# Attention in slots of 64 queries over 192 keys with the sink as a score column, and x norms summed by ScalarE from a copy of x by tokens

## The chip, the cores and the metric

The kernel runs on one core of a Trainium2 chip. The metric is the device time of one execution in microseconds. The engines are called as the profile calls them: PE (TensorE, with PEld for its weight loads), ACT (ScalarE), DVE (VectorE), POOL (GpSimd) and SP (SyncE, which issues nearly all DMAs). L245 is line 245 of the kernel; where the changed kernel is meant, the text says so, since its lines are shifted.

## The reference, cut to what matters

Two pre-norm residual layers over 4096 tokens of 1024 features in float32, and a last norm. Layer A is sliding-window attention: 16 query heads in 4 groups, each with one key/value head, 64 features a head, a window of 128 keys, and one learned sink per head. Layer B is a pooling mixer. Both are gated by SiLU(z).

```
def attn_layer(h, w_in, sinks, w_out):            # h = rmsnorm(x, g)
    q, k, v, z = split(h @ w_in)                  # 1024, 256, 256, 1024 columns
    o = swa_with_sinks(q, k, v, sinks)
    return (o * silu(z)) @ w_out                  # added to x

# swa_with_sinks, per block of 128 queries and 256 keys (block before, own block)
s = einsum('bnqhgd,bnkhd->bnhgqk', qb, kc) / sqrt(64)
diff = qi + 128 - kj
s = where((diff >= 0) & (diff < 128) & not_pad, s, -inf)
m = max(max(s), sink)
p = exp(s - m);  p = p / (sum(p) + exp(sink - m))
o = einsum('bnhgqk,bnkhd->bnqhgd', p, vc)
```

## The kernel before, in words

**Products.** Accuracy is that of float32: each operand is split into a high and a low part of a rounded 32-bit type, and a product takes three passes (high·high, high·low, low·high). A unit is 256 output columns of a projection for one group of 512 tokens: 48 matmuls of 128x512 (`in_piece`, L245), for v 96 of 128x256 (`v_piece`, L255).

**Order.** Layer A goes through 8 groups. A group is 14 units: k, q0 to q3 (one per kv head), v, z0 to z3, and the four out units of the group before. Beside them run 16 attention iterations, one for each kv head j and block b of 128 queries: `it_scores`, then `it_turn` (transposes of the probabilities), then `it_pv`. All work is put into a list of events with a due time in units (`at(t, fn, ...)`, offsets in the dictionary `T`), which is sorted and emitted in that order; each engine executes its part of it in order. Accumulators and scores live in PSUM: `mm` (two buffers) for the units, `pt` (two buffers) which the transposes, the PV result and the norm sums share, and `s` (one buffer) for the scores.

**Scores.** `it_scores` makes for each of the 4 heads of j a 128x256 score tile by two matmuls (L338: q high and low stacked in the 128 rows, against k high and then k low, which stand in both halves of `kt`). The window holds exactly 128 of the 256 keys, so DVE writes the block before over the masked half (`copy_predicated`, L344) and only 128 columns go on: DVE takes the maximum (L349) and the negative bias with the sink (L350), ACT the exponentials with their sums (L353), DVE and ACT add the sink's exponential (L354 to L356), POOL multiplies by the reciprocal (L358).

**PV.** `it_turn` transposes the 4 tiles into one `pt` buffer (L365), ACT rounds it (L371), DVE takes the low parts (L372, L376), and POOL zeroes by `affine_select` (L382 to L386) the keys that belong to the other block. `it_pv` multiplies with v: two matmuls of 512 columns (L396) and two of 256 (L398, L399).

**Norms.** A group's x is loaded by features (`xt`, 4 DMAs of 512 KB, L163). For the norm of the next group ACT squares 8 chunks, DVE adds them (L178), the sum is split, and PE sums over the features with a matrix of ones (`total`, L198, two matmuls); two small DMAs bring the result into another shape, `spread` (L205) makes the reciprocal root and broadcasts it by two further DMAs. Then `x_scale` (DVE) and `h_chunk` (ACT, DVE) make h. The output of layer A goes through the same `square`, `rstd`, `total` and `spread` (keys 8 to 15) for the norm of layer B.

**Layer B** follows from about 1610 us on in 4 pairs of groups. What prepares its first pair (loads of x, `h_load`; `h_scale`; the sums that its products need, `factor`) is placed within the last units of layer A.

## Time and profile before

| | us |
|---|---|
| median of 3 runs | 2634.66 (2632.97 to 2638.23) |
| the profiled execution | 2637.84 |
| its span | 2635.8 |
| PE busy | 2542.3 (96%) |
| DVE busy | 1796.4 (68%) |
| ACT busy | 1082.9 (41%) |
| POOL busy | 661.7 (25%) |

How to read it: a row of a timeline gives the start and the length of a run of equal instructions on one engine, then engine, line, operation, tiles written and read, the shape and xcount; what stands in brackets is the idle time before it and who ended it. A row of the groups gives busy time, the mean of one in ns, and the idle time before. The modelled end of a matmul overlaps the next one's start, so a pace is read from start to start.

### The profile page before, as it was taken

The page shows a single profiled execution, that of the slowest core. Times are in us where ns is not written, and L with a number is a line of the kernel's source. Part 1 is how long each engine was busy: PE and PEld are TensorE (multiplying, and loading weights), DVE is VectorE, ACT ScalarE, POOL GpSimd, SP SyncE. Part 2 cuts the span into 40 slices and gives each one's busy share as a digit, 9 for nine tenths or more (in the row PEclk, how much of TensorE's full clock was granted, in tenths as well). Part 3 has the DMA queues.
Part 4 walks back from the last instruction along what each step waited for, and adds up shares of the span by engine and source line. Part 5 has one row for each costly group of instructions (what it writes and reads, how often), then busy time and mean ns, then how long its engine had stood idle before and what let it go on. Part 6 is the DMA issues. An engine that isn't in the chain of part 4 may idle for free. (4 is left out here: it accounts for less than half of the span.)

```text
span 2635.8 us, 35629 instructions
## 1 busy us (share of the span) xinstructions
PE 2542.3 (96%) x12362; PEld 2120.9 (80%) x12362; DVE 1796.4 (68%) x3074; ACT 1082.9 (41%) x2774; POOL 661.7 (25%) x1048
## 2 busy tenths in 40 slices
PE   7999999999999999999999999999999999999997
PEld 5878878878888788778788877888878877887886
DVE  6898778778777678677677667547645655655544
ACT  5556455455455455455455443123313231331221
POOL 0354444344354354444344340000000000000000
PEclk9999999999999999999999999999999999999998
DMA  7755765775775774765775547667678668758752
GB/s 280 291 190 188 260 226 186 265 234 185 261 263 187 244 244 178 258 231 175 261 236 178 187 166 287 198 206 259 195 251 275 221 220 284 257 180 274 245 203 96
DMA packets 166284, 594.66 MB, mean 226 GB/s; under 512 B 22981, under 2 KB 33221, under 8 KB 137434
## 3 DMA queue, kind: packets, MB, share of 16 engines
q1 hardware_dynamic: 166106, 592.40, 65.8%
q8 instruction: 98, 1.61, 0.2%
q14 instruction: 80, 0.66, 0.1%
HBM read 474.81 MB, written 117.53 MB: 225 GB/s over the span
## 5 line engine op out<-in xcount | busy, mean ns | idle before, releaser
L245 PE MATMUL mm<-h,w 128*128 128x512 f32 x3456 | 853.8, 396 | 2.8 <-DVE sz L321 1.9
L245 PEld LDWEIGHTS mm<-h,w 128*128 128x128 f32 x3456 | 634.7, 190 | 125.2 <-DVE sz L321 2.4
L245 PE MATMUL mm<-a,w 128*128 128x512 f32 x1536 | 368.9, 394 | 5.1 <-DMA w<-wparts 5.1
L245 PEld LDWEIGHTS mm<-a,w 128*128 128x128 f32 x1536 | 285.0, 189 | 61.9 <-DVE xr L729 5.5
L358 POOL TENSOR_TENSOR P<-P,sm 128x512 f32<-128x512 f32 x128 | 140.6, 1099 | 452.6 <-DVE sm L357 340.9
L353 ACT ACTIVATE P<-s,nm 128x128 f32<-128x128 f32 x512 | 180.9, 366 | 130.1 <-DVE nm L350 126.0
L384 POOL TENSOR_SCALAR_AFFINE_SELECT m<-m 64x512 fp32r<-64x512 f32 x256 | 187.5, 733 | 82.7 <-DVE m L376 80.0
L712 POOL TENSOR_TENSOR rs<-ms,mhalf 128x4 f32<-128x4 f32 x7 | 7.0, 1006 | 738.4 <-DVE ms L711 738.4
L382 POOL TENSOR_SCALAR_AFFINE_SELECT m<-m 64x256 fp32r<-64x256 f32 x256 | 110.7, 432 | 276.7 <-ACT m L371 268.3
L338 PEld LDWEIGHTS s<-kt,q 128*128 128x128 f32 x1024 | 140.0, 191 | 39.0 <-ACT P L353 19.2
L338 PE MATMUL s<-kt,q 128*128 128x256 f32 x1024 | 152.0, 287 | 16.9 <-ACT P L353 11.7
L404 ACT COPY tmp<-po 64x256 f32<-64x256 f32 x256 | 93.9, 367 | 149.2 <-DVE o L405 93.0
L405 DVE TENSOR_TENSOR o<-po,tmp 64x256 f32<-64x256 f32 x256 | 107.7, 421 | 45.1 <-ACT tmp L404 39.0
L386 POOL TENSOR_SCALAR_AFFINE_SELECT m<-m 64x256 fp32r<-64x256 f32 x256 | 134.1, 524 | 13.5
L290 DVE TENSOR_TENSOR q<-mm,q 64x512 fp32r<-64x512 f32 x128 | 88.1, 688 | 62.0 <-ACT q L289 59.9
L289 ACT CAST q<-mm 64x512 fp32r<-64x512 f32 x128 | 74.3, 581 | 103.2 <-DVE q L290 57.6
L376 DVE TENSOR_TENSOR m<-pT,m 64x256 fp32r<-64x256 f32 x256 | 107.9, 422 | 7.9
L344 DVE COPY_PREDICATED s<-mask,s 128x512 f32<-128x512 int8 x124 | 85.6, 690 | 36.2 <-PE s L338 35.1
L353 ACT ACTIVATION_READ_ACCUMULATOR P<-s,nm 128x1 f32 x512 | 104.5, 204 | 0.0
L372 DVE TENSOR_TENSOR m<-pT,m 128x512 fp32r<-128x512 f32 x128 | 88.1, 688 | 21.5 <-ACT m L371 17.8
L178 DVE TENSOR_TENSOR sq<-sq,sr 128x512 f32<-128x512 f32 x112 | 87.9, 784 | 20.1 <-ACT sr L177 18.0
L371 ACT CAST m<-pT 128x512 fp32r<-128x512 f32 x128 | 75.4, 589 | 58.2 <-PE pT L365 31.1
(356 smaller groups left out, 4617.8 us busy)
## 6 DMA issues: line engine op xcount, KB each, us to landing
w<-wparts SPq DMA_DIRECT2D x196, 1024.0 KB
wparts<-w SPq DMA_DIRECT2D x28, 1024.0 KB
xt<-in_xt SPq DMA_DIRECT2D x32, 512.0 KB
res<-in_xt SPq DMA_DIRECT2D x32, 512.0 KB
x<-res SPq DMA_DIRECT2D x32, 512.0 KB
xr<-x SPq DMA_DIRECT2D x32, 512.0 KB
w_u<-part_u SPq DMA_DIRECT2D x56, 256.0 KB
w_z<-part_z SPq DMA_DIRECT2D x56, 256.0 KB
```

The lines of the kernel that those rows point to most:

```text
L245: nc.tensor.matmul(ps[:, c], w[:, wl, k % 4, 128 * c:128 * c + 128], rhs(k, hl), start=(k == 0 and i == 0), stop=(k == NK - 1 and i == 2))
L290: nc.vector.tensor_sub(q[64 - r:128 - r, h], src, f32(q[r:r + 64, h]))
L338: nc.tensor.matmul(ps[:, h], qs[s, j][:, h, 128 * b:128 * b + 128], kt[:, j, hl, 128 * b:128 * b + 256], start=(hl == 0), stop=(hl == 1))
L353: nc.scalar.activation(P[:, h], sc[:, h], AF.Exp, bias=nm[:, h:h + 1], scale=SCALE, accum_out=sm[:, h:h + 1])
L358: nc.gpsimd.tensor_mul(P, P, sm.unsqueeze(2).to_broadcast([128, 4, 128]))
L372: nc.vector.tensor_sub(m1[:, 1], pv, f32(m1[:, 0]))
L376: nc.vector.tensor_sub(m2[other, :, cols], pv[own, :, cols], f32(m1[own, 0, :, cols]))
L382: nc.gpsimd.affine_select(out=m2[own, :, cols], in_=f32(m1[own, 0, :, cols]), compare_op=ALU.is_ge, fill=0.0, **keep)
L384: nc.gpsimd.affine_select(out=mv, in_=f32(mv), compare_op=ALU.is_ge, fill=0.0, **drop)
L386: nc.gpsimd.affine_select(out=mv, in_=f32(mv), compare_op=ALU.is_ge, fill=0.0, **keep)
L404: nc.scalar.copy(tmp[d:d + 64], pv[e:e + 64, :, r])
L405: nc.vector.tensor_add(o[d:d + 64, :, 128 * b:128 * b + 128], pv[d:d + 64, :, r], tmp[d:d + 64])
```

## The change

1. **Scores in slots.** A slot is 64 queries of two heads, against the 192 keys that their windows can reach. An iteration has 4 slots (two pairs of heads, two halves of the block) and still 8 matmuls, of 192 columns instead of 256. q is evacuated times -1/8, so scores are negative; ACT writes minus the sink as one more column beside each slot's 128 kept columns; a minimum over 129 columns gives the bias, and the exponentials' sums hold the sink. L350, L354, L355 and L356 go.
2. **PV.** Six matmuls of 256 columns in place of two of 512 and two of 256. The copies of v that this needs are made by POOL (`vn`), ACT and two DMAs a group; the second half of `kt` is filled by 4 DMAs a group in place of ACT and DVE copies.
3. **Norms of x.** For groups 1 to 7, x is loaded a second time by tokens (`xm`, 4 DMAs of 512 KB a group), and ACT squares each with its sum (`accum_out`). The DVE adds, the split, the `total` matmuls and the two small DMAs go for them. The `xt` pool has 2 buffers instead of 4; two of a group's four `xt` are loaded in the last unit, and the scaling of chunks 4 to 7 stands at the end of the unit or after it.
4. **Order.** q2 stands before the last out unit and q3 before z1 in groups 1 to 6; scores are spaced evenly by about 0.8 unit; the norm sums of the output stand 0.9 unit after the end of out3 and no longer at 9.45 units after the group's start.
5. **Start and first pair of B.** The constants are loaded earlier; the preparation of B's first pair is spaced by 6 units for each of its four parts.

The core of the diff:

```diff
+    def xm_load(s, b):
+        t = sp.tile([128, D], F32, tag="xt", bufs=2, name=f"xm{s}_{b}")
+        nc.sync.dma_start(t, xm[s, b])
+        xts[s, "m", b] = t
+
+    def xm_square(s, b):
+        if b == 0:
+            rss[s] = const.tile([128, NB], F32, tag="mr", bufs=2, name=f"mr_{s}")
+        t = xts.pop((s, "m", b))
+        nc.scalar.activation(t, t, AF.Square, accum_out=rss[s][:, b:b + 1])
...
+    def k_twice():
+        for r in (0, 1):
+            v = f32(kt).rearrange("p (c r) l t -> p r c l t", r=2)[:, r]
+            for l in range(2):
+                nc.sync.dma_start(v[64 - 64 * r:128 - 64 * r, :, l, 128:], v[64 * r:64 * r + 64, :, l, 128:])
...
-            nc.scalar.copy(q[r:r + 64, h], src)
-            nc.vector.tensor_sub(q[64 - r:128 - r, h], src, f32(q[r:r + 64, h]))
+            src = ps[r:r + 64, h // 2].rearrange("p (t x) -> p t x", x=64)
+            dst = q[:, h // 2, :, h % 2]
+            nc.scalar.mul(dst[r:r + 64], src, -SCALE)
+            nc.vector.scalar_tensor_tensor(dst[64 - r:128 - r], src, -SCALE, f32(dst[r:r + 64]), op0=ALU.mult, op1=ALU.subtract)
...
     def it_scores(s, j, b):
         ps = rpsum.tile([128, 4, 256], F32, tag="s", bufs=1, name=f"s{s}_{j}_{b}")
-        for h in range(4):
-            for hl in range(2):
-                nc.tensor.matmul(ps[:, h], qs[s, j][:, h, 128 * b:128 * b + 128], kt[:, j, hl, 128 * b:128 * b + 256],
-                                 start=(hl == 0), stop=(hl == 1))
...
+        nc.scalar.copy(view(ps, 1, [(512, 2), (447, 2)]), nsink[:, j].unsqueeze(2).to_broadcast([128, 2, 2]))
+        for c in range(2):
+            for u in range(2):
+                t = 128 * b + 64 * u
+                for hl in range(2):
+                    nc.tensor.matmul(ps[:, 2 * c + u, 2 - 2 * u:194 - 2 * u], qs[s, j][:, c, 2 * b + u].rearrange("p r x -> p (r x)"), kt[:, j, hl, t:t + 192],
+                                     start=(hl == 0), stop=(hl == 1))
...
+        nc.vector.tensor_reduce(mx.rearrange("p (c u) -> p c u", c=2), view(ps, 1, [(512, 2), (319, 2), (1, 129)]), axis=AX.X, op=ALU.min)
+        P = sp.tile([128, 4, 136], F32, tag="P", bufs=2, name=f"P{s}_{j}_{b}")
+        for i in range(4):
+            nc.scalar.activation(P[:, i, 0:129], view(ps, 1 + 512 * (i // 2) + 319 * (i % 2), [(1, 129)]), AF.Exp,
+                                 bias=mx[:, i:i + 1], scale=-1.0, accum_out=sm[:, i:i + 1])
...
-        for hl in range(2):
-            nc.tensor.matmul(po, vm[:, b, j], m1[:, hl].rearrange("p h q -> p (h q)"), start=(hl == 0), stop=False)
-        ph = po.rearrange("p (h q) -> p h q", h=4)
-        nc.tensor.matmul(ph[:, :, 0:64], vp[:, b, j], m2[:, :, 0:64], start=False, stop=False)
-        nc.tensor.matmul(ph[:, :, 64:128], vc[:, b, j], m2[:, :, 64:128], start=False, stop=True)
+        for u, (v, before) in enumerate(((vm, vp), (vn, vq))):
+            for hl in range(2):
+                nc.tensor.matmul(pu[:, u], v[:, b, j], mu[:, u, hl], start=(hl == 0), stop=False)
+            nc.tensor.matmul(pu[:, u], before[:, b, j], m2[:, u], start=False, stop=True)
...
-            order = [("k", 0), ("q", 0), ("v", 0), outs[0], outs[1], ("q", 1), outs[2], outs[3], ("z", 0), ("q", 2),
-                     ("z", 1), ("q", 3), ("z", 2), ("z", 3)]
+            order = [("k", 0), ("q", 0), ("v", 0), outs[0], outs[1], ("q", 1), outs[2], ("q", 2), outs[3], ("z", 0),
+                     ("q", 3), ("z", 1), ("z", 2), ("z", 3)]
...
-            for r, fn in ((9.0, rstd), (9.45, total), (9.75, spread)):
-                at(base + r, fn, NG + s - 1)
+            for r, fn in ((0.1, rstd), (0.9, total), (1.2, spread)):
+                at(base + order.index(("out", 3)) + 1 + r, fn, NG + s - 1)
```

**Where instructions move.** On PE in group 4, from the last products of q1 (`mm` of w_1 with h_7) to the first scores of kv head 1 (`s_1_0`); the `mm` with `a` is an out unit. Before:

```order
L245 MATMUL mm_8887<-h_7_8097,w_1_8817 128x512 x6
L245 MATMUL mm_9032<-a_3_7387,w_0_8894 128x512 x12
L198 MATMUL ms_9047<-sr_8980,ones_r 128x512
L198 MATMUL ms_9047<-sl_8981,ones_r 128x512
L245 MATMUL mm_9032<-a_3_7647,w_0_8894 128x512 x12
L245 MATMUL mm_9032<-a_3_8111,w_1_8972 128x512 x6
L396 MATMUL po_0_3_9081<-m_4_0_3_9005,vm 128x512 x2
L398 MATMUL po_0_3_9081<-m_4_0_3_9006,vp 128x4x64
L399 MATMUL po_0_3_9081<-m_4_0_3_9006,vc 128x4x64
L245 MATMUL mm_9032<-a_3_8111,w_1_8972 128x512 x6
L245 MATMUL mm_9032<-a_3_8550,w_1_8972 128x512 x6
L338 MATMUL s_1_0_9103<-kt,q_1_9023 128x256 x8
```

Now:

```order
L267 MATMUL mm_8515<-h_7_7883,w_1_8431 128x512 x6
L267 MATMUL mm_8667<-a_3_7251,w_0_8522 128x512 x12
L432 MATMUL po_0_2_8703<-m_4_0_2_8613,vm 128x2x128
L375 MATMUL s_1_0_8676<-kt,q_1_8658 128x192 x4
L432 MATMUL po_0_2_8703<-m_4_0_2_8613,vm 128x2x128
L433 MATMUL po_0_2_8703<-m_4_0_2_8614,vp 128x2x128
L432 MATMUL po_0_2_8703<-m_4_0_2_8613,vn 128x2x128 x2
L433 MATMUL po_0_2_8703<-m_4_0_2_8614,vq 128x2x128
L398 MATMUL pT_0_3_8715<-ident,P_0_3_8583 128x128 x4
L267 MATMUL mm_8667<-a_3_7573,w_0_8522 128x512 x2
L375 MATMUL s_1_0_8676<-kt,q_1_8658 128x192 x4
```

Between the end of q1 and the first scores that read it stood 42 matmuls of 512 columns, the norm's two and a PV; now 12 and one of 256. The norm sums of x are gone from the place, and the scores are issued in two halves, one for each pair of heads.

On PE in group 3, around the norm sums of the output (`ms` with `ones_r`). Before:

```order
L338 MATMUL s_1_3_7344<-kt,q_1_6971 128x256 x8
L245 MATMUL mm_7377<-h_0_5928,w_0_7211 128x512 x6
L365 MATMUL pT_1_2_7394<-ident,P_1_2_7268 128x128 x4
L245 MATMUL mm_7377<-h_1_5980,w_0_7211 128x512 x6
L396 MATMUL po_1_1_7417<-m_3_1_1_7295,vm 128x512 x2
L398 MATMUL po_1_1_7417<-m_3_1_1_7296,vp 128x4x64
L399 MATMUL po_1_1_7417<-m_3_1_1_7296,vc 128x4x64
L245 MATMUL mm_7377<-h_2_5999,w_0_7211 128x512 x6
L245 MATMUL mm_7377<-h_3_6010,w_0_7211 128x512 x6
L245 MATMUL mm_7377<-h_4_6019,w_1_7324 128x512 x6
L245 MATMUL mm_7377<-h_5_6028,w_1_7324 128x512 x2
L198 MATMUL ms_7439<-sr_7390,ones_r 128x512
```

Now:

```order
L432 MATMUL po_1_2_7174<-m_3_1_2_7084,vm 128x2x128 x2
L433 MATMUL po_1_2_7174<-m_3_1_2_7085,vp 128x2x128
L432 MATMUL po_1_2_7174<-m_3_1_2_7084,vn 128x2x128 x2
L433 MATMUL po_1_2_7174<-m_3_1_2_7085,vq 128x2x128
L398 MATMUL pT_1_3_7186<-ident,P_1_3_7060 128x128 x4
L267 MATMUL mm_7122<-h_4_5851,w_1_7044 128x512 x6
L267 MATMUL mm_7122<-h_5_5861,w_1_7044 128x512 x6
L267 MATMUL mm_7122<-h_6_5942,w_1_7044 128x512 x6
L267 MATMUL mm_7122<-h_7_5946,w_1_7044 128x512 x6
L220 MATMUL ms_7229<-sr_7131,ones_r 128x512
L220 MATMUL ms_7229<-sl_7132,ones_r 128x512
```

The two `pt` buffers are taken in turn, so the sums need the buffer of the transposes two places ahead (before: `pT_1_2`, with `po_1_1` after it; now: `po_1_2`, with `pT_1_3` after it). 20 matmuls of 512 columns stood between the last user of `pt` and the sums, and 24 do now; a different tile is waited for.

On SP at the end of layer A, from the broadcasts of the first pair's norm (`bch`) on. Before:

```order
L719 DMA bch_16313<-rsq_120 128x512
L719 DMA bch_16313<-rsq_121 128x512
L724 DMA xr_3_16316<-x_0_76 128x1024
L724 DMA xr_3_16316<-x_1_77 128x1024
L724 DMA xr_2_16319<-x_0_76 128x1024
L724 DMA xr_2_16319<-x_1_77 128x1024
L724 DMA xr_1_16322<-x_0_76 128x1024
L724 DMA xr_1_16322<-x_1_77 128x1024
L724 DMA xr_0_16325<-x_0_76 128x1024
L724 DMA xr_0_16325<-x_1_77 128x1024
L422 DMA x_7_83<-res_0_16138 128x1024
L151 DMA w_0_16384<-wparts_0_2862 128x2048
```

Now:

```order
L754 DMA bch_15718<-rsq_120 128x512
L754 DMA bch_15718<-rsq_121 128x512
L759 DMA xr_3_15721<-x_0_76 128x1024
L759 DMA xr_3_15721<-x_1_77 128x1024
L759 DMA xr_2_15752<-x_0_76 128x1024
L759 DMA xr_2_15752<-x_1_77 128x1024
L457 DMA x_7_83<-res_0_15582 128x1024
L158 DMA w_0_15786<-wparts_0_2734 128x2048
L450 DMA res_2_15736<-in_xt 128x1024
L759 DMA xr_1_15815<-x_0_76 128x1024
L759 DMA xr_1_15815<-x_1_77 128x1024
L158 DMA w_1_15838<-wparts_1_2826 128x2048
```

Eight loads of `xr` stood ahead of the next weights (`w_0`); four do now, and the other four stand between later weight loads.

196 lines of the change are left out of this document (99 added, 97 removed).

## The prediction

> **What bounds the kernel now.** I read the page's sums first, then the windows by stage (width; then busy time and instruction count of PE, PEld, DVE, ACT, POOL; granted PE clock; DMA share; GB/s).
>
> ```profile
> span 2635.8 us, 35629 instructions
> PE 2542.3 (96%) x12362; PEld 2120.9 (80%) x12362; DVE 1796.4 (68%) x3074; ACT 1082.9 (41%) x2774; POOL 661.7 (25%) x1048
> ...
> 215.30:1394.00 1178.70, 1148.77 (x5883) 967.73 (x5882) 885.74 (x1729) 598.83 (x1741) 499.75 (x772) 0.99 0.66 226
> 1610.00:2636.00 1026.00, 999.76 (x4414) 824.18 (x4414) 589.72 (x766) 270.48 (x467) 10.16 (x36) 0.99 0.68 226
> ```
>
> PE is busy 1148.77 of 1178.70 us in groups 1 to 6 (the third row), where the change has nearly all its edits; the next engine, DVE, has 885.74 there, 75%. The last row, layer B's 1026 us, is touched only in its first preparation. So the time is the sum of PE's own paces and of the moments at which it waits. The waits, by the view of waits on PE (total, times, longest):
>
> ```profile
> PE ms L198 <- DVE m L376: 12.6, 6, 2.5
> PE s L338 <- ACT P L353: 11.7, 11, 3.0
> PE pT L365 <- DVE m L376: 5.2, 8, 1.5
> PE mm L245 <- DMA w<-wparts: 5.1, 1, 5.1
> PE po L396 <- POOL m L384: 2.7, 5, 1.4
> PE po L396 <- DVE o L405: 1.6, 3, 1.0
> ```
>
> These 38.9 us are all that waits can give back; the paces must give the rest. They come from the timeline, from start to start:
>
> ```profile
> 1001.87 3.00 PE L245 MATMUL mm<-h,w 128*128 128x512 f32 x12
> 1004.70 0.62 PE L396 MATMUL po<-m,vm 128*128 128x512 f32 x2
> ...
> 1019.49 1.12 PE L338 MATMUL s<-kt,q 128*128 128x256 f32 x8
> 1020.45 0.63 PE L396 MATMUL po<-m,vm 128*128 128x512 f32 x2
> ...
> 1021.15 4.47 PE L255 MATMUL mm<-w,h 128*128 128x256 f32 x36
> ```
>
> 512 columns take (1004.70 − 1001.87)/12 = 0.236 us, 256 columns (1020.45 − 1019.49)/8 = 0.120, a whole PV 1021.15 − 1020.45 = 0.70. Halving the columns thus saves 0.116, and each column costs 0.116/256 = 0.00045.
>
> **The change part by part.** The profiled execution took 2637.84, span and 2.0 around it; the median of the runs is 2634.66, so 3.2 are taken off at the end.
>
> *Scores.* 1024 matmuls go from 256 to 192 columns. No row has 192. If columns alone decide, one takes 0.120 − 64 × 0.00045 = 0.091, and the edit gives 1024 × 0.029 = 30 us; if the narrowing gains nothing, 0. What stands between is the weight load that each matmul needs, seen where the moving operand is a single column:
>
> ```profile
> 2609.26 0.98 PEld L770 LDWEIGHTS msl<-ones,sq 128*128 128x128 f32 x8
> 2610.15 1.02 PEld L752 LDWEIGHTS last<-set_3out_B,w_3o 128*128 128x128 f32 x8
> ```
>
> Eight loads with nothing wide beside them step at (2610.15 − 2609.26)/8 = 0.111. I take 0.111, since the new matmul also brings its own 128x128 weights: **−9.2** (0 to −30). The Trainium skill, "TensorE: Matmul & The Clock Gate", section "Back-to-back issue gap", gives sustained paces of about 81 ns at 128 columns and 131 at 512. An estimate by it is 89 ns at 192 columns and −31 us; but this trace has 0.236 at 512. [...]
>
> *PV.* Six of 256 columns take 6 × 0.120 = 0.72 against 0.70, 128 times: **+2.6** (0 to +4 if the strided operand costs 0.01 a PV more).
>
> *Norm sums of x.* Seven groups lose two matmuls of 512: 14 × 0.236 = **−3.3**. The sums of the output stay, and the 12.6 us of the first wait are six times theirs. One of them:
>
> ```profile
> 715.68 0.60 PE L365 MATMUL pT<-ident,P 128*128 128x128 f32 x4
> ...
> 722.73 0.60 ACT L371 CAST m<-pT 128x512 fp32r<-128x512 f32 x1
> ...
> 724.08 0.87 DVE L376 TENSOR_TENSOR m<-pT,m 64x256 fp32r<-64x256 f32 x2
> ...
> 725.10 0.47 PE L198 MATMUL ms<-sr,ones_r 128*128 128x512 f32 x1 [2.19 <-DVE m L376]
> ```
>
> The sums take the `pt` buffer of transposes written at 715.68; ACT reaches their cast only at 722.73, behind a gate and four exponentials, DVE's subtractions end at 724.95, and PE had come 2.19 us earlier. In the new order the sums take the buffer of a PV result, with 24 matmuls of 512, 5.7 us, after the transposes that follow it. Its readers are two copies on ACT and two additions on DVE, in place of a cast and three subtractions. I count 10 of the 12.6 as gone: **−10** (0, if ACT is as late there, to −12.6).
>
> *Score chain and other waits.* Per iteration DVE and ACT do less between scores and exponentials:
>
> ```profile
> L344 DVE COPY_PREDICATED s<-mask,s 128x512 f32<-128x512 int8 x124 | 85.6, 690 | 36.2 <-PE s L338 35.1
> L349 DVE TENSOR_REDUCE mx<-s 128x4 f32<-128x512 f32 x128 | 88.0, 688 | 2.4
> L350 DVE SCALAR_TENSOR_TENSOR nm<-mx,nsink 128x4 f32<-128x4 f32 x128 | 22.4, 175 | 1.6
> L353 ACT ACTIVATE P<-s,nm 128x128 f32<-128x128 f32 x512 | 180.9, 366 | 130.1 <-DVE nm L350 126.0 <-PE mm L245 3.1
> L353 ACT ACTIVATION_READ_ACCUMULATOR P<-s,nm 128x1 f32 x512 | 104.5, 204 | 0.0
> L376 DVE TENSOR_TENSOR m<-pT,m 64x256 fp32r<-64x256 f32 x256 | 107.9, 422 | 7.9
> L178 DVE TENSOR_TENSOR sq<-sq,sr 128x512 f32<-128x512 f32 x112 | 87.9, 784 | 20.1 <-ACT sr L177 18.0
> ```
>
> The selection goes from 4 x 128 to 4 x 64 columns a row, 0.69 to about 0.42 (as L376 with 256 elements), the 0.175 of L350 goes, and ACT's write of the sink, on 128x2x2, stands before the matmuls. It joins ACT's queue: behind it wait the scores, behind them everything on PE. Between score groups there are at least 7.7 us of PE work in the new order, 6.1 in the old (matmuls counted at the paces above), and the chain itself needs 0.42 + 0.69 + 4 × (0.366 + 0.204) = 3.4. DVE loses 49 × 0.784 = 38 us of L178 over the kernel and 128 × 0.27 = 35 of the selection. The other waits, 11.7 + 5.2 + 2.7 + 1.6 = 21.2, are of an engine that comes late by 1 to 3 us; I count not quite half as gone: **−9** (+11 to −21: as much new again, or all).
>
> *A new wait behind q1.* From the last products of q1 to the first scores that read q there were 42 matmuls of 512 and are 12 and one of 256, 3.0 us. Evacuating q takes four ACT casts and four DVE subtractions:
>
> ```profile
> 925.76 0.58 ACT L289 CAST q<-mm 64x512 fp32r<-64x512 f32 x1 [3.22 <-PE mm L245]
> ...
> 927.61 0.58 ACT L289 CAST q<-mm 64x512 fp32r<-64x512 f32 x1
> ...
> 929.26 0.69 DVE L290 TENSOR_TENSOR q<-mm,q 64x512 fp32r<-64x512 f32 x1
> ```
>
> The first pair was done 929.95 − 925.76 = 4.2 us after it began, with other work between; undisturbed it is two casts and a subtraction, some 1.9. The scores come in two halves now, and the first needs one pair: a wait of 0 to 1.2, and some again for the second half. I take 1 us for 6 groups: **+6** (0 to +12).
>
> *Loads of x by tokens.* 28 more transfers of 512 KB. For one of that size:
>
> ```profile
> 389.19 0.33 SPq L163 DMA_DIRECT2D xt<-in_xt  x1
> ...
> 393.63 0.63 ACT L171 ACTIVATE sq<-xt 128x512 f32<-128x512 f32 x1
> ```
> ```profile
> 67.94 1.26 SPq L163 DMA_DIRECT2D xt<-in_xt  x2
> ...
> 73.65 0.63 ACT L177 ACTIVATE sr<-xt 128x512 f32<-128x512 f32 x1 [5.29 <-DMA xt<-in_xt]
> ```
>
> The first landed within 4.4 us, since its square started without a wait; the second, beside the start's other loads, in 5.7. In the new program the squares are emitted 1.5 to 5 us of PE work behind their loads, which have two buffers, and so wait for the square two before. ACT may stand for 1 to 3 us a group, mostly inside the 7.7 − 3.4 = 4.3 us of slack between scores; 7 groups at 0.7: **+5** (0 to +20; a loss of more is the third rival). The `kt` and v copies, six DMAs a group, cost nothing while v's unit (96 matmuls of 256, 11.5 us) and the out units stand ahead of their readers; without that cover they would cost a landing of 4.4 us a group. POOL's 64 new copies find it idle for 679 of 1179 us.
>
> *The tail.* The one DMA wait of 5.1:
>
> ```profile
> 1590.38 6.17 SPq L724 DMA_DIRECT2D xr<-x  x8
> ...
> 1608.37 0.38 SPq L151 DMA_DIRECT2D w<-wparts  x1
> ...
> 1610.42 2.04 PE L245 MATMUL mm<-a,w 128*128 128x512 f32 x4 [5.07 <-DMA w<-wparts]
> ```
>
> Eight loads go ahead of the weights, four now: **−3.5** (0 to −5). The start and the last group's order: **+2** (−3 to +5).
>
> Sum: −9.2 + 2.6 − 3.3 − 10 − 9 + 6 + 5 − 3.5 + 2 = −19.4, that is 2637.8 − 19.4 = 2618.4 profiled, and less 3.2 **2615** in the runs.
>
> **The rivals.**
>
> *R1, columns decide.* The load hides under the matmul before, and 192 columns take 0.091: 20 us more are gained, **2595**. For it: 256-column matmuls at 0.120, with a load each, are 0.009 above the load's step, so columns and loads do overlap. Against: no row with a load for each matmul steps faster than 0.111.
>
> *R2, waits are only renamed.* The sums wait for the next late tile, the new wait behind q1 takes 1 to 2 us a group, and the tail keeps its 5: −9.2 + 2.6 − 3.3 + 10 = 0, **2635**. For it: the six waits at L198 end with the same ACT and DVE that stay in the path. Against: by the rows above DVE alone has 38 + 35 + 22 = 95 us less to do.
>
> *R3, slower: ACT stands at `xm`.* If each 512 KB takes the 5.7 us of the start or more (the DMA share is already 0.66, and the change adds 4 MB a group: 2 of `xm`, 1 of `kt`, 1 of v), ACT waits at each of four squares some 2.5 us, 10 a group. The stretch has one score gap, whose slack of 4.3 covers part; from there on exponentials and casts come late and PE waits for the rest: 5.7 × 7 = 40, **2655**. It decides once a landing exceeds about 4.5 us. Against: 4.4 at 389 with no wait, at a share like today's.
>
> *R4, narrow matmuls in two passes.* The profile shows twice the emitted instructions for some plain float32 products of 128 columns:
>
> ```profile
> L785 PE MATMUL bcl<-ident,rs_l x16: 271/349/583, 2614.6 to 2628.8; 128*128 128x128 f32 x16
> ```
>
> 16 stand there for 8 emitted. Would the rounded type with fewer than 256 columns go the same way, each score matmul would take about 0.22: 1024 × 0.10 more, **2720**. Against: the rounded types are made to avoid just that, and the transposes of 128 columns (L365, x4 for 4) do not double.
>
> **How the numbers follow.** Forecast 0.60 (its own range 2602 to 2629: the ends of the wait terms), R1 0.14, R2 0.13, R3 0.09, R4 0.04. The range 2588 to 2638 takes in the forecast, R1 and R2 whole; above it lie R3 and R4 (0.13), below it R1 together with all waits gone (0.06). A measurement of this kernel tells about 0.2% (5.3 us) from no change. Faster by more: the forecast, R1 and a fifth of R2, 0.77; within: most of R2, 0.10; slower: R3 and R4, 0.13.
>
> **What would show it.** The step of L375 rows, start to start, near 0.111 (0.091 for R1, 0.2 for R4). No L220 row with a wait above 0.5 us. L375 rows that wait for q's second cast or subtraction, some 1 us in each of six groups. ACT squares of `xm` with a DMA named as releaser: under 3 us a group, 10 for R3. PE's busy time down by about 10. DVE's busy time lower by over 95. I am wrong if a wait with a new name on PE sums to more than 15 us, or if layer B's 1026 us change.

## The result: slower by 4.0%

| us | before | after |
|---|---|---|
| median of the runs | 2636.44 | 2741.77 (2732.12 to 2746.55) |
| the profiled execution | 2637.84 | 2741.26 |
| its span | 2635.8 | 2739.2 |

The ratio is 1.0396, with its interval 1.0364 to 1.0427. The forecast was 2615, with a range to 2638: wrong in sign, by 127 us.

The page of the changed kernel, its sums:

```profile
span 2739.2 us, 35678 instructions
PE 2602.2 (95%) x12604; PEld 2159.3 (79%) x12604; DVE 1626.7 (59%) x2546; ACT 1066.1 (39%) x2728; POOL 701.1 (26%) x1122
```

and its windows by stage, with the columns as in the prediction (group 0; the stretch of time that the prediction used for groups 1 to 6; from there to 1668; and the rest, with layer A's last out units and layer B):

```profile
60.00:215.30 155.30, 137.59 (x754) 117.36 (x753) 102.13 (x167) 79.75 (x212) 61.78 (x93) 0.93 0.72 246
215.30:1394.00 1178.70, 1119.17 (x5730) 940.10 (x5729) 706.72 (x1236) 550.08 (x1602) 500.15 (x784) 0.97 0.69 232
1394.00:1668.00 274.00, 260.74 (x1351) 216.57 (x1349) 165.60 (x301) 128.20 (x391) 119.68 (x191) 0.98 0.62 205
1668.00:2739.00 1071.00, 1042.88 (x4568) 849.76 (x4568) 614.29 (x793) 279.44 (x483) 13.67 (x44) 0.99 0.67 226
```

In the second row DVE is down to 706.72 from 885.74 and ACT to 550.08 from 598.83. Part of this is only that less work falls into the same stretch of time. Over the same work, from group 1's first v product to group 7's (1254.0 us after, 1176.6 before), DVE is busy 758.15 us against 885.81 and ACT 583.43 against 598.62: still less, as the change promises. In the second row PE is down as well, to 1119.17 from 1148.77, and its granted clock from 0.99 to 0.97. PE did less in the same time because it stood, and it ran slower after it had stood. The waits on PE (total, times, longest):

```profile
PE s L375 <- ACT s L370: 33.9, 22, 4.7
PE po L432 <- POOL m L417: 14.8, 26, 1.5
PE pT L398 <- DVE m L410: 12.8, 8, 4.2
...
PE mm L277 <- DMA w<-wparts: 10.7, 6, 3.0
...
PE po L433 <- POOL m L419: 3.9, 7, 1.0
...
PE s L375 <- DVE q L315: 2.9, 6, 0.5
```

The 12.6 us of the norm sums (`ms`) are gone. In their place the scores wait 33.9 us for the sink that ACT writes into their tile, where before they waited 11.7 for ACT's exponentials. One such wait, followed back on all engines:

```profile
1001.59 0.83 SPq L533 DMA_DIRECT2D w_u<-part_u  x2
...
1009.12 0.41 ACT L130 CAST part_u<-sum_u 128x256 fp32r<-128x256 f32 x1 [5.71 <-DMA w_u<-part_u]
...
1009.56 0.42 DVE L131 TENSOR_TENSOR part_u<-sum_u,part_u 128x256 fp32r<-128x256 f32 x1 [5.43 <-ACT part_u L130]
1009.87 0.59 ACT L314 ACTIVATE q<-mm 64x512 fp32r<-64x512 f32 x1
...
1012.42 0.37 ACT L387 ACTIVATE P<-s,mx 128x129 f32<-128x129 f32 x1 [0.20 <-DVE mx L384]
...
1014.31 1.05 POOL L390 TENSOR_TENSOR P<-P,sm 128x516 f32<-128x516 f32 x1 [11.23 <-DVE sm L389]
...
1014.96 0.59 ACT L404 CAST m<-pT 128x512 fp32r<-128x512 f32 x1
...
1015.44 0.17 ACT L370 COPY s<-nsink 128x4 f32<-128x4 f32 x1
...
1015.66 1.14 PE L375 MATMUL s<-kt,q 128*128 128x192 f32 x8 [2.45 <-ACT s L370]
```

`part_u` has nothing to do with this iteration. While layer A runs, both kernels split layer B's weights into high and low parts (ACT casts, DVE subtracts, SP stores them to memory for later); a part has one of two buffers, and is free again when its store has landed. The two stores of 1001.59 had not, so ACT, which executes in order, stood 5.71 us at the head of its queue; DVE stood 5.43 behind it, and POOL, which needs the sums of the exponentials, had been idle for 11.23. The late exponentials are followed by a cast and by the sink, and PE waits 2.45 us for it. The parts are the same in both kernels; the stands are not. The view of waits on ACT, after:

```profile
ACT part_u L130 <- DMA w_u<-part_u: 40.1, 13, 5.7
ACT part_z L130 <- DMA w_z<-part_z: 31.3, 12, 5.9
ACT part_o L130 <- DMA wo<-part_o: 26.9, 9, 6.4
ACT xm L186 <- DMA xm<-in_xm: 23.7, 12, 5.1
```

and before:

```profile
ACT part_u L123 <- DMA w_u<-part_u: 23.5, 16, 3.4
ACT part_o L123 <- DMA wo<-part_o: 21.1, 11, 3.9
ACT part_z L123 <- DMA w_z<-part_z: 18.1, 15, 3.4
ACT part_o L123 <- DMA w_z<-part_z: 8.5, 4, 4.0
```

98 us in three rows against 71 in four, and the longest 6.4 against 4.0; with the small rows of that view it is 112 against 80. Of the 73 us that PE waits for other engines from group 1 to the end of layer A, 60 begin within 14 us after ACT or DVE stood at a DMA; before, 24 of 35. These stands and the 14 us behind them cover about 44% of that stretch after and 40% before.

What a long wait costs beyond itself shows in PE's timeline of group 0:

```profile
104.66 1.04 PE L375 MATMUL s<-kt,q 128*128 128x192 f32 x8
105.53 0.42 PE L432 MATMUL po<-m,vm 128*128 128x256 f32 x2
...
113.67 1.09 PE L398 MATMUL pT<-ident,P 128*128 128x128 f32 x4 [4.21 <-DVE m L410]
114.41 4.96 PE L267 MATMUL mm<-h,w 128*128 128x512 f32 x11
119.21 0.40 PE L432 MATMUL po<-m,vm 128*128 128x256 f32 x2
```

Eight matmuls of 192 columns take 105.53 − 104.66 = 0.87 us, 0.109 each. Behind the wait of 4.21, eleven of 512 columns take 119.21 − 114.41 = 4.80, 0.436 each instead of 0.23: half pace, from the first matmul behind the wait on. The window over these 4.8 us:

```profile
113.70:118.50 4.80, 4.80 (x14) 3.93 (x15) 1.62 (x5) 1.59 (x4) 3.62 (x6) 0.50 0.97 405
```

The granted clock is 0.50, and the trace's record of it has 0.50 from 112.3 to 119.1, so from within the wait on. The Trainium skill, "TensorE: Matmul & The Clock Gate", section "The HAM clock gate (the "warmup" mystery)", says that about 3.4 us of idleness throttle the array to half its clock and that about as long a stretch of work releases it, in windows that run freely. The trace agrees with the length: between the kernel's start and its end, each stretch at 0.50 in the two kernels' records lasts 3.4 or 6.8 us. It does not agree with 3.4 us of idleness as the condition. There are 22 such stretches after, 109 us in all, and 8 before, 34 us, and ten of the 22 came behind waits that were each under 2 us. One of them, with the window behind it:

```profile
1071.16 1.14 PE L375 MATMUL s<-kt,q 128*128 128x192 f32 x8 [0.32 <-ACT s L370]
1073.06 0.50 PE L432 MATMUL po<-m,vm 128*128 128x256 f32 x2 [0.76 <-POOL m L417]
...
1074.24 0.50 PE L432 MATMUL po<-m,vn 128*128 128x256 f32 x2 [0.24 <-POOL m L417]
...
1074.90:1078.30 3.40, 3.40 (x11) 2.90 (x11) 0.13 (x1) 1.62 (x3) 0.00 (x0) 0.50 1.02 411
```

Waits of 0.32, 0.76 and 0.24 us were enough here. In the kernel before, the scores at 899.16 came behind a wait of 3.04 us, and the clock over the next 3.8 us was 1.00. So several short waits close together can halve the clock, and one long wait need not.

From start to start of all matmuls I took the time apart for six kernels: the nominal steps (0.227, 0.120, 0.111 and 0.109 us for 512, 256, 192 and 128 columns), what a step lasts longer because PE waited, steps over 1.5 times nominal without a wait (half clock), and the small excess that is left. The last four kernels are explained below.

| us | before | after | a_pad640 | b_pad384 | a_nosplit | ap_tied |
|---|---|---|---|---|---|---|
| nominal steps | 2490.1 | 2481.0 | 2481.0 | 2490.1 | 2481.0 | 2481.0 |
| waits | 88.8 | 142.1 | 149.1 | 77.3 | 113.8 | 120.9 |
| half clock | 25.6 | 65.0 | 61.5 | 18.4 | 43.9 | 43.3 |
| small excess | 12.5 | 32.8 | 9.1 | 33.5 | 33.4 | 10.4 |
| first to last matmul | 2617.0 | 2720.9 | 2700.7 | 2619.3 | 2672.0 | 2655.7 |

From before to after: −9 of steps, +53 of waits, +39 of half clock, +20 of small excess: +104. The row of half clock holds more than its name says: of these steps 46 us after and 15 before lie in the stretches that the trace records at 0.50; the others are at the kernel's start, and short stops within scores and PV. So some 32 of the +39 are half clock. By groups it is (from one group's first v product to the next one's):

| us | 0 | 1 | 2 | 3 | 4 | 5 | 6 |
|---|---|---|---|---|---|---|---|
| before | 171.1 | 195.0 | 194.9 | 192.8 | 197.2 | 198.1 | 198.5 |
| after | 186.3 | 210.9 | 211.6 | 208.6 | 209.6 | 208.5 | 204.7 |
| a_nosplit | 189.0 | 219.8 | 220.8 | 191.4 | 191.1 | 192.5 | 191.1 |
| b_nosplit | 170.1 | 197.6 | 207.6 | 194.4 | 189.2 | 189.8 | 189.2 |
| ap_tied | 187.2 | 189.4 | 202.5 | 202.3 | 194.8 | 204.0 | 204.3 |

The loss, 10 to 17 us a group, begins in group 0 and is there in each of them until group 5; group 6 loses 6. In the names of the experiments a_ is the changed kernel with an edit, b_ the kernel before with one, ap_ the changed kernel with the padding of the first experiment. Each ratio is to the kernel before on the same chip; the runs come from several chips, on which the kernel before took 2632 to 2638, so a difference between the medians of two variants can be off by some 5 us.

### The profile page after: what moved, and what is told of

Its sections match the earlier page's. It is cut to its first block, busy times and chain, and to the rows that moved or that the text cites. A ratio compares the mean times of both kernels' runs of the same rounds, so it can differ in the third digit from the quotient of the medians.

```text
span 2739.2 us, 35678 instructions
## 1 busy us (share of the span) xinstructions
PE 2602.2 (95%) x12604; PEld 2159.3 (79%) x12604; DVE 1626.7 (59%) x2546; ACT 1066.1 (39%) x2728; POOL 701.1 (26%) x1122
## 4 chain that ended last, share of the span: by engine, by line
PE 50%; DVE 15%; DMA 14%; issue 13%; ACT 7%; POOL 1%; SPq 1%; ACTq 0%; POOLq 0%; DVEq 0%
PE mm L267 23%; DMA fin<-x 3%; PE mm L277 3%; PE s L375 2%; DMA out<-fin 2%; ACT P L387 2%; DMA w<-wparts 2%; DMA w_u<-part_u 2%; PE po L432 1%; DVE q L315 1%; PE pT L398 1%; DMA xm<-in_xm 1%; PE X_3u L620 1%; PE X_3z L620 1%; DVE m L410 1%
## 5 line engine op out<-in xcount | busy, mean ns | idle before, releaser
L267 PEld LDWEIGHTS mm<-h,w 128*128 128x128 f32 x3456 | 652.8, 194 | 140.9
L390 POOL TENSOR_TENSOR P<-P,sm 128x516 f32<-128x516 f32 x128 | 135.5, 1059 | 463.4 <-DVE sm L389 459.1
L387 ACT ACTIVATE P<-s,mx 128x129 f32<-128x129 f32 x512 | 182.2, 370 | 140.9 <-DVE mx L384 138.2
L375 PE MATMUL s<-kt,q 128*128 128x192 f32 x1024 | 142.5, 281 | 43.2 <-ACT s L370 33.9
L315 DVE SCALAR_TENSOR_TENSOR q<-mm,q 64x512 fp32r<-64x512 f32 x128 | 88.1, 689 | 73.9 <-ACT q L314 72.6
L314 ACT ACTIVATE q<-mm 64x512 fp32r<-64x512 f32 x128 | 76.0, 593 | 138.0 <-DVE q L315 83.0
L277 PE MATMUL mm<-w,h 128*128 128x256 f32 x768 | 100.6, 290 | 10.7 <-DMA w<-wparts 10.7
L277 PEld LDWEIGHTS mm<-w,h 128*128 128x128 f32 x768 | 97.9, 197 | 12.6 <-DMA w<-wparts 11.9
L380 DVE COPY_PREDICATED s<-mask,s 128x256 f32<-128x256 int8 x128 | 54.4, 425 | 89.8 <-PE s L375 79.0
L387 ACT ACTIVATION_READ_ACCUMULATOR P<-s,mx 128x1 f32 x512 | 104.5, 204 | 0.0
```

The costliest lines, as they stand in the source:

```text
L267: nc.tensor.matmul(ps[:, c], w[:, wl, k % 4, 128 * c:128 * c + 128], rhs(k, hl), start=(k == 0 and i == 0), stop=(k == NK - 1 and i == 2))
L277: nc.tensor.matmul(ps[:, b], hts[s, k][:, hl, 128 * b:128 * b + 128], wtiles[U, k // 4][:, wl, k % 4], start=(k == 0 and i == 0), stop=(k ...
L315: nc.vector.scalar_tensor_tensor(dst[64 - r:128 - r], src, -SCALE, f32(dst[r:r + 64]), op0=ALU.mult, op1=ALU.subtract)
L375: nc.tensor.matmul(ps[:, 2 * c + u, 2 - 2 * u:194 - 2 * u], qs[s, j][:, c, 2 * b + u].rearrange("p r x -> p (r x)"), kt[:, j, hl, t:t + 19 ...
L387: nc.scalar.activation(P[:, i, 0:129], view(ps, 1 + 512 * (i // 2) + 319 * (i % 2), [(1, 129)]), AF.Exp, bias=mx[:, i:i + 1], scale=-1.0, ...
L390: nc.gpsimd.tensor_mul(P[:, :, 0:129], P[:, :, 0:129], sm.unsqueeze(2).to_broadcast([128, 4, 129]))
```

## The experiments

### 1. The small excess: where the tiles lie

The small excess has a plain sign in layer B, which the change does not touch, and which took 7 us longer. The groups view shows the same 96 matmuls of 512 columns, before

```profile
L634 PE MATMUL X_1o<-set_1out_B,w_1o 128*128 128x512 f32 x96 | 24.4, 389 | 0.0
```

and after:

```profile
L669 PE MATMUL X_1o<-set_1out_B,w_1o 128*128 128x512 f32 x96 | 24.7, 392 | 0.0
```

Step by step, every one takes 0.226 to 0.228 before; after, 20 of the 96 take 0.236 to 0.239 and 36 more at least 0.229, and the mean goes from 0.2267 to 0.2303. The change removes constants, 640 bytes in each partition, so the pool behind them (weights, the operands of layer B) starts 640 bytes lower, and its place modulo 512 turns from 384 to 256. The first run adds an unused tile of 640 bytes to the changed kernel:

```diff
+    pad = const.tile([128, 160], F32, name="pad")
+    nc.vector.memset(pad, 0.0)
```

> The changed kernel with one unused tile of 640 bytes a partition among the constants, so that the pool of the left side (weights, the operands of layer B) starts again at the byte where it started before (5504 instead of 4864); nothing else moves. Theory 'addresses': in layer B, whose work is unchanged, a quarter to a half of the 512-column matmuls of some products step at 0.238 us instead of 0.227, in the same share of each product, and PE's small excess is 33 us against 12; with the old start both go back, so the run is 15 to 25 us shorter than the changed kernel (2741 to about 2720), layer B's part 7 us of it. Rival 'another chip or another run': the paces stay as they were in the changed kernel's profile, or are gone without the tile; time unchanged within 5 us.

Measured: 2727.13, ratio 1.0358 (1.0342 to 1.0373), 14.6 less than after (10 by the two ratios). The row of X_1o, whose mean step is 0.2267 again:

```profile
L671 PE MATMUL X_1o<-set_1out_B,w_1o 128*128 128x512 f32 x96 | 24.4, 389 | 0.0
```

The mirror image adds 384 bytes (`[128, 96]`) to the kernel before, so that its tiles lie modulo 512 where those of after do.

> The kernel before with one unused tile of 384 bytes a partition among the constants, so that the left pool starts at 5888, which leaves the same rest by 1024 as the changed kernel's 4864. Theory 'addresses': 512-column matmuls of layer B step at 0.238 in a quarter to a half of some products, and the time rises by 12 to 25 us, to about 2655. Rival 'another chip or another run': the time stays within 5 us of the kernel before.

Measured: 2647.28, ratio 1.0061 (1.0044 to 1.0077).

```profile
L636 PE MATMUL X_1o<-set_1out_B,w_1o 128*128 128x512 f32 x96 | 24.7, 392 | 0.0
```

The small excess goes 32.8 to 9.1 in the one and 12.5 to 33.5 in the other, and the time follows it by 10 to 15 us down and 15 up. (In the profiled execution of b_pad384, the fastest of its four, shorter waits hide most of it, as the table shows: 2619.3 against 2617.0.) So some 10 to 20 of the 105 us come from the addresses alone, with not one instruction of the computation different. Which operand is read more slowly, and why, no run here tells.

### 2. The sink, the xm squares and the added transfers

The sink's own place is the nearest suspect: it stands behind the exponentials and, mostly, behind a cast. Here it is written for the next iteration right behind this one's exponentials:

```diff
+        i = 16 * s + 4 * j + b + 1
+        if 16 < i < 16 * NG:
+            sink_tile(i // 16, i % 16 // 4, i % 4)
```

> The changed kernel with the sink column of the next iteration written where the exponentials of this one end, from group 1 on, and no longer where the next scores are issued. Theory 'sink in ACT's queue': the waits of PE for that write sum to 40 us, and in 24 of them the write stood behind a copy and a cast that came after the exponentials; they shrink by 10 to 24 us, and the time by 15 to 35 with the slow clock that follows long waits. Rival 'ACT is late anyway' (it is held at DMA landings before the exponentials): the waits keep their sum within 5 us, and the time within 8.

Measured: 2734.14, ratio 1.0389 (1.0372 to 1.0406), within the rival's 8 us of after. The waits on PE:

```profile
PE po L443 <- POOL m L428: 29.1, 35, 5.0
PE s L383 <- ACT s L372: 17.2, 14, 3.0
...
PE po L444 <- POOL m L430: 4.8, 8, 0.9
```

The sink's waits halve, 33.9 to 17.2, as the theory has it, but those for POOL rise from 18.7 to 33.9. What is late is all of ACT's and DVE's work, and PE meets it at the next place where it reads some.

The `xm` loads and squares with due times two units later (`sqA=4.5`, `rsA=7.5` in place of 2.5 and 5.5):

> The changed kernel with the loads of x by tokens, their squares and the norm's spread 2.0 units later in each group (loads from 3.2 instead of 1.2 units on), when the buffers they take have long been free. Theory 'SP is held': SP stands 53 us in 12 waits before those loads for the last h chunks, with weight loads and stores of prepared weights queued behind it, and ACT then stands at the squares (24 us) and at the stores (111 us); the waits of PE for weights (12 us) go and ACT's DMA waits fall by half, time 20 to 35 us less. Rival 'the loads cost bandwidth, not order': SP's wait goes, the time stays within 8 us.

Measured: 2741.09, ratio 1.0413 (1.0398 to 1.0429). Nothing changes, but the run does not test what it was made for. The due times moved and the built program hardly did: in the traces 27 of the 28 squares stand behind the same attention iteration as in the changed kernel, most of them behind the last three of a group. ACT's stands at `xm` stay (22.0 us against 23.7), and so do SP's 53 before these loads. What the third rival's mechanism costs therefore stays open; ACT stands there for 3.4 us a group, and the rival needs 10.

Two more kernels ask for the bytes of the added transfers. The first loads an eighth of each `xm` and makes about an eighth of the `kt` and v copies; norms and attention are then computed from incomplete data, and ACT's squares keep nearly their length:

```diff
-        nc.sync.dma_start(t, xm[s, b])
+        nc.sync.dma_start(t[:, 0:128], xm[s, b][:, 0:128])
...
-        nc.sync.dma_start(f32(vp[64:128, 1:]), upper)
+        nc.sync.dma_start(f32(vp[64:128, 1:, 0, 0:64]), upper[:, :, 0, 0:64])
```

> The changed kernel with its three kinds of added transfers cut to an eighth of their bytes (x by tokens, the second half of kt, the copies of v); their number, order and all instructions stay, the output is not the reference's. Theory 'bytes': these 4 MB a group lengthen the landings of everything else (weights in group 0, stored parts, xt), and ACT and DVE stand there in order; group 0 loses its 15 us and groups 1 to 6 half of theirs, 30 to 55 us in all (to 2685 to 2710). Rival 'sink, PV and order, whatever the traffic': less than 12 us.

Measured: 2731.45, ratio 1.0378 (1.0353 to 1.0404).

The second makes the `kt` and v copies on ACT and DVE in place of DMAs:

```diff
-                nc.sync.dma_start(v[64 - 64 * r:128 - 64 * r, :, l, 128:], v[64 * r:64 * r + 64, :, l, 128:])
+            nc.scalar.copy(kt[d:d + 64, j, 0, 128:], f32(kt[r:r + 64, j, 0, 128:]))
+            nc.vector.tensor_copy(kt[d:d + 64, j, 1, 128:], f32(kt[r:r + 64, j, 1, 128:]))
```

> The changed kernel with the second half of kt and the copies of v made by ACT and DVE (8 more copies of 0.62 on ACT, 8 and 8 of some 0.5 on DVE a group) and not by six DMAs a group; output unchanged. Theory 'bytes': 2 of the 4 added MB go, 10 to 30 us less. Rival: ACT and DVE pay 4 to 9 us a group at the group's start, -5 to +15.

Measured: 2735.74, ratio 1.0393 (1.0376 to 1.0409). By the medians these are 10 and 6 us less than after, by the ratios 5 and 1. The 30 to 55 us that the first expectation gave to the bytes are not there: the traffic is a side matter.

### 3. The new order, and the norms alone

The changed kernel with the old unit order, score times and place of the output's norm sums:

```diff
-            order = [("k", 0), ("q", 0), ("v", 0), outs[0], outs[1], ("q", 1), outs[2], ("q", 2), outs[3], ("z", 0),
-                     ("q", 3), ("z", 1), ("z", 2), ("z", 3)]
+            order = [("k", 0), ("q", 0), ("v", 0), outs[0], outs[1], ("q", 1), outs[2], outs[3], ("z", 0), ("q", 2),
+                     ("z", 1), ("q", 3), ("z", 2), ("z", 3)]
...
-            for r, fn in ((0.1, rstd), (0.9, total), (1.2, spread)):
-                at(base + order.index(("out", 3)) + 1 + r, fn, NG + s - 1)
+            for r, fn in ((9.0, rstd), (9.45, total), (9.75, spread)):
+                at(base + r, fn, NG + s - 1)
```

> The changed kernel with the order of units, the times of the scores and the place of the output's norm sums as they were before (q2 after z0, q3 after z1, scores of kv heads 1 to 3 from 6.8, 10.2 and 13.2 units on, sums at 9.45 units); slots, sink column, PV in six matmuls and norms by tokens stay. Theory 'order': PE waits for work that the new order brings too early or too late for ACT; of the 85 us that the addresses do not explain, 40 to 80 go (2741 to 2660 to 2700), the wait at the norm sums (12 us) comes back. Rival 'the work itself' (sink in ACT's queue, copies of v, loads): the time stays within 15 us.

Measured: 2772.11, ratio 1.0501 (1.0463 to 1.0539).

```profile
PE s L376 <- ACT s L371: 45.6, 22, 5.9
...
PE ms L221 <- DVE m L411: 19.1, 7, 4.3
```

Both expectations missed: the old order in the changed kernel is worse by 30 us, though ACT's stands at the parts fall from 112 us to 96, and it brings the norm sums' waits back. The reverse, the kernel before with the new order (the same lines with + and − exchanged, and the new score times):

> The kernel before with the new order of units, times of scores and place of the output's norm sums, and nothing else of the change. Theory 'order': 40 to 80 us longer than before (2632 to about 2690), with PE waiting for ACT's exponentials. Rival 'the work itself': the 12 us of waits at the norm sums go and nothing comes, 2620 to 2635.

Measured: 2650.88, ratio 1.0053 (1.0035 to 1.0072).

```profile
PE po L395 <- POOL m L383: 20.3, 14, 3.1
...
PE pT L364 <- POOL P L357: 10.0, 9, 4.5
```

Here the norm sums wait no more, and the 12.6 us come back at POOL: the second rival's renaming, in the kernel before. ACT's stands at the parts rise from 80 us to 107. The kernel before with the norms by tokens alone (the `xm` loads and squares, two `xt` buffers, the late `xt` loads and scalings):

```diff
+                at(base + T["sqA"] + T["sqAd"] * n - 1.3, xm_load, s + 1, n)
+                at(base + T["sqA"] + T["sqAd"] * n, xm_square, s + 1, n)
+                at(base + L + (-3.2, -3.0, -0.74, -0.49)[n], xt_load, s + 1, n)
```

> The kernel before with the norms of x by tokens alone (28 more loads of 512 KB, squares with sums on ACT, two xt buffers with the late loads and the late scaling of chunks 4 to 7). Theory 'loads and late scaling' (DVE stands 15 us at xt, ACT 24 us at xm, and the largest waits of PE lie at the ends of groups, where both happen): 20 to 45 us longer than before. Rival: the 14 matmuls and DVE's additions go and little else happens, -8 to +8.

Measured: 2652.62, ratio 1.0061 (1.0036 to 1.0086). In the kernel before, the new order alone costs 14 us and the norms alone 16: neither is the gain that the waits it removes had promised, and neither is the loss that its theory foresaw (40 to 80, and 20 to 45).

### 4. The parts of layer B's weights

If the stands at the stores of parts are the cause, taking them away must give the time back. This kernel leaves out the split: raw blocks of the same size are stored in place of the parts, so ACT and DVE have no work on them and cannot stand, while the traffic stays; layer B then works with these blocks.

```diff
-                split_sb(t[:, 0], t[:, 1], raw[:, c])
-                nc.sync.dma_start(wout[key[1]][2 * hf + c // 2][:, :, c % 2], f32(t))
+                nc.sync.dma_start(wout[key[1]][2 * hf + c // 2][:, :, c % 2], raw[:, 2 * (c // 2):2 * (c // 2) + 2])
```

> The changed kernel with the preparation of layer B's weights cut down: the parts are stored as they are loaded or summed, without ACT's cast and DVE's subtraction and without their two buffers, so the output is not that of the reference; bytes and number of the stores stay. It takes away the stands of ACT at those stores (111 us after, 78 before). Theory 'ACT held at stores': the waits of PE for the sink write, POOL and the transposes fall to a third, and the time by 40 to 70 us. Rival 'order or work': they fall by less than a third, the time by less than 20.

Measured: 2692.68, ratio 1.0209 (1.0183 to 1.0236), 49 less than after. The same edit in the kernel before:

> The kernel before with the parts stored as they are loaded or summed, without ACT's cast and DVE's subtraction; the output is not the reference's. It gives the price of that work and its stands in the old order, beside 49 us in the changed kernel. Theory 'ACT held at stores, and the old order had room for it': less than 25 us. Rival 'the work costs the same in both': 40 to 60 us.

Measured: 2621.67, ratio 0.9954 (0.9938 to 0.997), 12 less. So the same parts cost some 12 us in the old arrangement and 49 in the new. The table by groups says more. In groups 3 to 6, where the parts' stores are all but over (the last is issued at 749.8 us), the changed kernel takes 191.1 to 192.5 us a group and the kernel before 189.2 to 194.4. The loss of 11 us a group that the two whole kernels show in these groups has shrunk to 1. So without parts the loss there is gone, but the changed attention gains nothing either, though it has some 1.2 us a group less of PE's steps (9.1 over the kernel); its addresses, 20 us of small excess over the whole, take about that back. In groups 1 and 2, into which nearly all stores now crowd, the changed kernel takes 220, and group 0 is as slow as ever; in all it is still some 70 us behind the kernel before without the split. With the thin transfers as well:

> The same with layer B's parts stored without ACT's cast and DVE's subtraction, as in the earlier run (2692.7). If stands of ACT and DVE at DMA landings are the whole loss beside the addresses, it comes to that run's counterpart of the kernel before, 2622, plus 15 for the addresses and minus 9 for the narrower scores: 2625 to 2650. Rival 'sink, PV and order': it stays above 2670.

Measured: 2705.39, ratio 1.028 (1.0258 to 1.0302); groups 4 to 6 at 191 again and group 3 at 196. The expectation that little but the addresses would be left (2625 to 2650) missed by 55 us. The crowd of stores does not need the added bytes.

Next, the same work with more room: the low part goes into the raw block and is stored from there, so four stores can be under way instead of two.

```diff
-                split_sb(t[:, 0], t[:, 1], raw[:, c])
+                split_sb(t[:, c % 2], raw[:, c].bitcast(F32R), raw[:, c])
```

> The changed kernel with four parts of layer B's weights under way instead of two: the high half goes into half a buffer, the low half is written over its source, and the two are stored by two DMAs of half the size. ACT's and DVE's work is the same; only the wait for the landing of the store two parts before becomes one for the store three or four before. Theory 'ACT held at stores': ACT's stands there (114 us) fall below half, PE's waits for the sink write, the transposes and POOL (76 us together) by 25 or more, the time by 25 to 60. Rival 'the work of the parts, or the attention itself': the stands fall, PE's waits stay within 10 us, the time within 12.

Measured: 2726.61, ratio 1.035 (1.0331 to 1.0369). With the padding of experiment 1:

> The same with the unused 640 bytes that put the left pool back to its old start. The two causes are independent if this is 12 to 18 us below the run with four parts alone; with theory 'ACT held at stores' it comes to 2665 to 2700, with the rival to about 2720.

Measured: 2708.20, ratio 1.0286 (1.0262 to 1.0309). By the medians the two gains add up, 15 to 18 from the addresses and 15 to 19 from the room, less than the 25 to 60 expected of the room. But ACT's stands at the parts only fell from 112 to 95 us, and 54 of these are now for loads of raw blocks, since a raw block is itself held until its stores land and so the next one is loaded late. The kernel before with more room:

> The kernel before with four parts under way. ACT stands 82 us at these stores there too, but PE's waits in groups 1 to 6 are only some 40 us: 0 to 15 us less than before by theory 'ACT held at stores', no change by the rival.

Measured: 2663.32, ratio 1.0113 (1.0095 to 1.0131): 30 slower, where 0 to 15 faster was expected, though ACT's stands at the parts fall from 80 to 58 us. Here the edit costs more than it gives; by which of its waits was not followed up.

Last, the same parts with the same two buffers, but in another place. That a part is due 0.8 unit behind its load does not set where it stands in the built program: in the changed kernel the first cast of a part ran at 348.4 us, in the middle of group 1, though its due time lies in group 2. Counted on ACT in the traces, between the exponentials of one iteration and those of the next, group 4's parts stand

```
before   0 0 0 4 0 1 2 6 2 2 4 1 0 0 0 0
after    0 0 0 0 0 0 0 1 3 4 4 4 5 2 1 1
ap_tied  2 2 2 1 2 2 2 1 1 1 1 1 1 1 1 1
```

Both kernels crowd them. Before, the crowd in groups 2 to 6 is one place of 4 to 7 and one of 6, with iterations of 2, and in some groups one of 4, behind; after, in groups 1 to 6 alike, five iterations running bring 3, 4, 4, 4 and 5, with two buffers for all. So this kernel ties each part to an iteration: its cast adds a bias that is zero times that iteration's sums, at most two parts an iteration. It also has the padding.

```diff
+        z = const.tile([128, 1], F32, tag="zero", bufs=2, name=f"zero{s}_{i}")
+        nc.vector.tensor_scalar(z, sm[:, 0:1], 0.0, None, op0=ALU.mult)
+        key, hf = sevens[4 * (s - 2) + i // 4]
+        for n in ([i % 4] if key[0] == "o" else [c for c in (2 * (i % 4), 2 * (i % 4) + 1) if c < 7]):
+            seven_part(key, hf, n, z)
```

> The changed kernel with the left pool at its old start, and with the 24 pieces of layer B's weights tied to the attention: at most two parts behind each iteration's reciprocal, held there by a zero made from that iteration's sums, which ACT adds in the cast (one more small DVE operation per iteration from group 2 on). All work and stores stay. In the changed kernel four to five parts stand between two iterations' exponentials in five to six iterations in a row, and two buffers let ACT do two in one landing. Theory 'where the parts stand': ACT no longer stands at stores (below 25 us instead of 118), groups 2 to 6 come near the 191 us of those without parts, and the time is 40 to 75 us below the run with the old start alone (2727 to 2652 to 2687). Rival 'the work of the parts, or the new attention': within 15 us of 2727.

Measured: 2675.73, ratio 1.0153 (1.0137 to 1.0169), 51 less than a_pad640, with all work kept, as the theory expected. The waits on PE, and ACT's at the parts:

```profile
PE pT L401 <- DVE m L413: 14.3, 9, 4.5
PE s L377 <- ACT s L372: 13.1, 14, 2.1
...
PE mm L269 <- DVE h L133: 7.6, 5, 1.6
...
PE mm L269 <- ACT h L132: 6.2, 3, 2.2
...
ACT part_z L542 <- DMA w_z<-part_z: 19.0, 6, 5.8
ACT part_u L542 <- DMA w_u<-part_u: 15.7, 4, 4.9
```

Against a_pad640, ACT's stands at the parts fall from 117 us to 35, the scores' waits for the sink from 36.3 to 13.1, half clock from 61.5 to 43.3. This is the strongest of the runs: beside one small DVE operation an iteration, and casts that add a bias, only the place of a side work changed, and half the loss went. How the 51 us divide between the stands and the crowd of casts and subtractions itself is not separated: this run and a_nosplit take both away, and a_slots4, which was to take the stands alone, left 95 us of them. The kernel before with the same tie:

> The kernel before with the same tie (the left pool at the same rest by 512 as before). Its groups 1 to 6 take 196 us with parts and 189.5 without. Theory 'where the parts stand': 10 to 30 us shorter than before, 2603 to 2623, and shorter than both kernels. Rival: within 6 us of before.

Measured: 2642.95, ratio 1.0033 (1.0019 to 1.0048). ACT's stands fall from 80 us to 6 there, yet the time, expected 10 to 30 us shorter, is 7 longer. These stands were shorter (4.0 at most), and it seems that PE did not meet most of them. The sum of an engine's stands is therefore no measure; what counts is whether one is longer than the slack behind it.

### What the runs leave open

Of the 105 us, 10 to 20 are the addresses and some 51 the place of the parts; ap_tied, with both mended, is still 40 slower than the kernel before. By the table of steps this is +32 of waits and +18 of half clock, less 9 of steps and 2 of small excess. By groups, 16 of it lie in group 0, which has no parts, and which is 15 to 18 longer in each variant of the changed kernel in that table. There the long wait of 4.21 us, shown above, follows a stand of ACT at the projections' own weights; in ACT's timeline:

```profile
104.33 0.17 ACT L370 COPY s<-nsink 128x4 f32<-128x4 f32 x1
106.92 1.05 ACT L130 CAST w<-wraw 128x1024 fp32r<-128x1024 f32 x1 [2.41 <-DMA wraw<-in_w_a_in]
107.99 0.59 ACT L314 ACTIVATE q<-mm 64x512 fp32r<-64x512 f32 x1
```

The same pattern, then, with other buffers; that it explains all of group 0 was not tested. The products that wait for h at the ends of groups (7.6 and 6.2 in ap_tied) point to the late loads and scalings of `xt`, which were tried only in b_norms, together with the loads by tokens. No version with the reference's whole work was faster than the kernel before.

## Why the prediction was wrong, by its own steps

- **Scores, −9.2: right.** The step is 0.109 to 0.114, near the weight load's 0.111. R1 (0.091) and R4 (0.2) are false.
- **PV, +2.6, and norm sums, −3.3: right** in kind: all nominal steps together fell by 9.1, and the forecast had −9.9 for the three.
- **The wait of the norm sums, −10: right there**, all 12.6 gone. b_order shows that the 12.6 are not thereby gained.
- **Behind q1, +6: in kind right, size too large:** 2.9 us on `q` itself, and none over 0.5.
- **`xm` and late loads, +5: the stand about as forecast, its price open.** ACT stands there for 23.7 us, 3.4 a group, a little over the 3 that the prediction named and far from the 10 that R3 needs. No run took these stands away. DVE's 15.0 us at late `xt` were not in the sum; their price stays open too.
- **The tail, −3.5: right in kind, too large.** The wait was 5.1 before; there are waits of 2.4 and 1.7 there after, so 1 us went.
- **Start and last group, +2: right.** The first v product begins at 62.9 us against 60.6, and from the last group's first v product to its last out product it is 226.2 against 225.9.
- **Score chain and other waits, −9, bounds +11 to −21: the step that failed.** It reasoned that the engines come earlier, since DVE has 95 us less to do. DVE had 170 us less over the kernel (1626.7 against 1796.4) and PE waited more: by 53 us in all, most of it here, and 10.7 at weights of the v units that land late. ACT and DVE are late where the parts of layer B's weights crowd and they stand at the heads of their queues for the stores; no saving of their own work on the scores shortens that, and spreading the parts alone gave back 51 us. The row that would have told it, `part_u` with 23.5 us of ACT and DMA as releaser, was in the view of waits on ACT before; the prediction uses that view for PE alone. And the new order moved the parts among the iterations, which the order of ACT's instructions would have shown.
- **A wait was costed at its own length.** In the changed kernel 15 waits were 2.5 us or longer (8 before), and within 6.5 us behind each PE lost 2.1 us more on the mean. Short waits close together halved the clock too. The term that was missing is the row of half clock, +39 us, of which some 32 lie in stretches recorded at 0.50.
- **Layer B unchanged: wrong,** by 7 us, and with it the term that no step had: the constants that go move the pool behind them. 10 to 20 us over the kernel.

The prediction named two signs that would make it wrong, a wait of a new name over 15 us and a change in layer B. Both came.

## What to carry to other kernels

On an engine that executes in order, list its waits for DMAs before counting its work: a side work with few buffers (here two, with landings of 2.0 to 6.1 us where the trace tells them) delays everything behind it, and an edit that only regroups such work between dependent steps can cost more than the edit saves. Cost a wait of PE above some 2.5 us at itself plus about 2 us of half clock, and look at the granted clock behind groups of shorter waits as well. Before a run with moved due times is read, look in its trace whether the instructions moved. When a change adds or removes a constant tile, compare a kernel padded back to the old addresses before judging the change.
